# Issue order of the inter-chunk products in the mLSTM part of a hybrid attention/mLSTM layer

## The chip, the cores and the metric

The kernel runs on one core of a Trainium2 chip. A core has five engines with their own instruction streams: TensorE (PE in the profile: matrix products and transposes, with PEld for loading the stationary operand), VectorE (DVE), ScalarE (ACT), GpSimd (POOL) and SyncE (SP), which here issues the DMAs. The engines wait for each other by semaphores. Products land in PSUM, from which VectorE and ScalarE read. The metric is the time of one execution on the device in microseconds; lower is better.

## The reference

One layer of a backbone with 1024 tokens of width 1024 and 256 context tokens. A modulated RMS norm and one input projection feed two head groups: windowed attention (8 query heads, 2 key/value heads, softmax with a sink) and a bidirectional chunkwise mLSTM (4 heads, keys and queries of 64, values of 128). Their outputs are concatenated and projected, and a SwiGLU sub-layer follows. The change is in the mLSTM. Its step for one chunk, cut to what is computed per direction:

```
s   = einsum('bhtd,bhsd->bhts', qc, kc) * w_intra
num = einsum('bhts,bhsv->bhtv', s, vc) + w_inter[..., None] * einsum('bhvd,bhtd->bhtv', C, qc)
den = s.sum(-1) + w_inter * einsum('bhd,bhtd->bht', n, qc)
h   = num / maximum(abs(den), exp(-m_t))[..., None]
```

The first product with `vc` is the intra-chunk part, the one with the carried state `C`, `n` the inter-chunk part. Forward and backward scans are summed.

## The kernel before

The kernel works in tiles of 128 tokens and takes chunks of 128 instead of 64. Its stages are: modulation vectors and input projections; the scan of the mLSTM states; the attention and mLSTM stage, about 290 to 450 us; the output projection; and the SwiGLU sub-layer, with its order written out by hand, to the end.

The attention and mLSTM stage runs over 16 items, one for each of 8 token blocks and 2 groups of four query heads. For an item, `Soft.scores` (L945) makes score products (L954, L955; results in the PSUM tile `s`, two buffers), which VectorE masks and reduces (L956); `Soft.norm` takes the exponential on ScalarE (L965), inverts the sum (L967) and scales on GpSimd (L970). This works two items ahead. `Values` transposes the probabilities (L984, into a PSUM bank called `pt`), splits them into a high and a low part (ScalarE L61, VectorE L62), and adds up products with the values (L994 with the high, L995 with the low part) in `po`; `out` copies and adds (L1002, L1003).

During items 0 to 7 the mLSTM of token block n = 0 to 7 is woven in. `ml_scores(n)` makes the products of keys and queries (L851), two heads at a time: 64 rows each, rows 0 to 63 and 64 to 127 in turn, into two PSUM banks; VectorE multiplies them into the weights `wl` (L856). `ml_values(n, d)`, for direction d = 0 (forward) and 1 (backward), takes two banks, `pv[0]` and `pv[1]`. Head 2j + hb (j and hb from 0 to 1) has its queries and its state in row half hb and adds up in bank `pv[hb]`. So there are four inter-chunk products (L866: scaled queries `qp` times state `cs`, 64 rows, 129 columns, of which the last is the denominator) and four intra-chunk products (L870: `wl` times `V`, 128 rows, 129 columns). Then VectorE makes the denominator (L875, L876 for each half, L877 once for both), and ScalarE (L882, forward) or VectorE (L884, backward) scales the result into `hs`, which frees the banks. `ml_norm` (L891 to L894) and `ml_out` (L900 transposes, L901) finish the block one item later.

All `pt` banks come from one pool of three buffers, so the banks of `ml_values` are those of earlier transposes and of the other direction: a product into a bank waits until what stood there has been read.

The order in this stage is not written out. `PLAN_ML` (L35) gives an order of calls in an item, and a scheduler of the compiler reorders the instructions of each engine by its own cost estimates. `tc.keep_in_program_order(x)` holds instruction x behind the ones that the program wrote before it on its engine. From L1077 on the order is fixed by `tc.manual_schedule()`.

Of the kernel before, what the change touches and what calls it, by code (L numbers as in the profile page):

```python
# [40 lines left out]
def body(tc, x, ctx, vecs, bcv, bada, gqm, gqf, wada, ws1, ws2, wt, wout, wfi, wfo,  # L41
         const, cosc, sinc, out):
    nc = tc.nc
    pe, act, dve, pool = nc.tensor, nc.scalar, nc.vector, nc.gpsimd
# [249 lines left out]
    for sec in (1, 0):  # L294
        pr = [pa.tile([4, 512], F32, name=f"pr{sec}{i}", tag="mm", bufs=4) for i in range(2)]
        for kt in range(KT):
# [17 lines left out]
            for n, (k, a, b) in enumerate(ops):  # L314
                if late and n < 2:
                    prep_t(1, True, (n,))
                for i in range(2):
                    r = pe.matmul(pr[i], a[:, k, :], b[:, i * 512:(i + 1) * 512], start=kt == 0 and n == 0,
                                  stop=kt == KT - 1 and n == len(ops) - 1)
# [19 lines left out]
        r = act.copy(r4[:, 0:512], pr[0])  # L339
# [79 lines left out]
    for i in range(NI):  # L419
# [7 lines left out]
        if i == 0:  # L427
            r = st[:, 13:14]
# [89 lines left out]
    def rows_of(n, d):  # L518
        s_ = n + 2 if d == 0 else 9 - n
        return s_, d * 64 + s_ * 4  # L520
# [166 lines left out]
    def state(d, s_):  # L687
        return c1t[d] if s_ == 1 else cst_[(s_ - 2) // 2][:, (s_ - 2) % 2, d]
# [135 lines left out]
    def bank():  # L824
        return pb.tile([P, 4, P], F32, name="pt", tag="pt", bufs=3)
# [32 lines left out]
    def ml_values(n, d):  # L858
        wt_, qp_, hs = wts[n], qps[n], hss[n][0]
        s_, r0 = rows_of(n, d)  # L860
        cs = state(d, s_)
        pv = [bank().rearrange("p a b -> p (a b)")[:, 0:258].rearrange("p (j v) -> p j v", j=2) for hb in range(2)]
        for j in range(2):
            for hb in range(2):
                r = slice(hb * 64, hb * 64 + 64)
                pe.matmul(pv[hb][:, j, :], qp_[r, d, j, :], cs[r, j, :], start=j == 0, stop=False,  # L866
                          skip_group_check=j > 0)
        for hb in range(2):
            for j in range(2):
                pe.matmul(pv[hb][:, j, :], wt_[:, d, 2 * j + hb, :], V[:, n, 2 * j + hb, :], start=False, stop=True,  # L870
                          skip_group_check=j > 0)
        dn = qa.tile([P, 2, 2], F32, name="dn", tag="dn", bufs=4)
        for hb in range(2):
            den = pv[hb][:, :, 128]
            dve.tensor_tensor(dn[:, hb], den, emcol[:, r0 + hb:r0 + 4:2], MAX)  # L875
            dve.scalar_tensor_tensor(dn[:, hb], den, -1.0, dn[:, hb], MUL, MAX)  # L876
        dve.reciprocal(dn, dn)  # L877
        for hb in range(2):
            for j in range(2):
                t = hs[:, 2 * j + hb]  # L880
                if d == 0:
                    act.activation(t, pv[hb][:, j, 0:128], AF.Copy, scale=dn[:, hb, j:j + 1])  # L882
                else:
                    dve.scalar_tensor_tensor(t, pv[hb][:, j, 0:128], dn[:, hb, j:j + 1], t, MUL, ADD)  # L884
# [149 lines left out]
    for i in range(NIT):  # L1034
# [8 lines left out]
        for k in (PLAN_ML if i < NT else PLAN13 if i == NIT - 3 else PLAN).split():  # L1043
            op, n = k[0], int(k[1:] or 0)
            if op == "w" and i + 1 < NT:
                ml_load(i + 1)
            elif op == "T" and n < b.nt:
                b.tr(n)
            elif op == "M" and n < b.nt:
                b.mm(n)  # L1050
            elif op == "O":
                b.out()
            elif op == "A" and a:
                a.scores(n)
            elif op == "N" and a:
                a.norm(n)
            elif op == "V" and i < NT:
                ml_values(i, n)
            elif op == "x" and i < NT:
                ml_norm(i)  # L1060
            elif op == "s" and i + 1 < NT:
                ml_scores(i + 1)
            elif op == "z" and 1 <= i <= NT:
                ml_out(i - 1)
            elif op == "l":
                for j in WLOADS.get(i, ()):
                    wout_load(j)
            elif op == "p" and 1 <= i <= KT:
                wout_split(i - 1)
            elif op == "m":  # L1070
                msplit(0, 0)
                ops_[0] = pb.tile([P, 1024], F32, name="op", tag="s", bufs=2)
            elif op == "P":
                omm(0, 0, range(n, n + 1))
# [634 lines left out]
    for p in range(4, HT):  # L1709
        j = p - 5  # L1710
# [265 lines left out]
```

## Time and profile before

| what | value |
| --- | --- |
| runs of the kernel, three | 1195.16, 1196.69, 1197.64 us |
| median | 1196.69 us |
| profiled execution, from its first to its last instruction | 1195.1 us |
| TensorE busy | 1174.9 us, 98% |
| VectorE busy | 818.4 us, 68% |
| ScalarE busy | 577.7 us, 48% |
| granted TensorE clock, mean | 0.998 |
| L866 in the trace | 128 records, from 305.1 to 410.6 us |
| L870 in the trace | 128 records, 300 ns in the mean |

Of the profiled execution only the span is given, so the span stands for its time. An fp32 product shows as two records, so the 64 products of L866 are 128 records. The ends of matrix products are modelled, and they overlap; what a product costs is read from one start to the next start. A line of the timeline has its start, its duration, engine, source line, operation, tiles (written <- read), shape and count, and in brackets the idle time before it with what ended it. A line of the chain of work has a start, the time that the chain spent there, and what. The timeline's "x4" merges four records in a row.

### The profile page before, as it was taken

Reading aid. Unit: us, or ns where it says so; the run is one execution under the profiler, and the core shown is the slowest. Engines: PE = TensorE matmul, PEld = TensorE weight load, DVE = VectorE, ACT = ScalarE, POOL = GpSimd, SP = SyncE. Lnnn points to the kernel's source line nnn. Section 1 sums busy time; section 2 is a strip of 40 time slices with the busy share of each in tenths; the row PEclk is TensorE's granted clock in tenths of the full one; section 3 lists DMA queues with packets and bytes.
Section 4 is the critical chain, followed back from the end, with each engine's and each line's share of the span. In section 5 each row is a group of like instructions: output and inputs, shape, how many; then the busy total and the mean of one; then the engine's idle time right before and its main releaser. Section 6 shows DMA issues by size and latency. Waiting matters only on the chain.

```text
span 1195.1 us, 16364 instructions
## 1 busy us (share of the span) xinstructions
PE 1174.9 (98%) x5881; PEld 967.6 (81%) x5881; DVE 818.4 (68%) x1437; ACT 577.7 (48%) x1075; POOL 150.6 (13%) x196
## 2 busy tenths in 40 slices
PE   9899999999999999999999999999999999999997
PEld 3799888877888778888788888888888888888886
DVE  5863768863888895458777678676777656544567
ACT  5743442232777785777534333333333335434443
POOL 1550001215444551000000000000000000000000
PEclk9999999999999999999999999999999999999999
DMA  9522955557878971521133565656553557665853
GB/s 366 193 71 59 374 195 172 179 141 238 191 216 243 313 229 44 203 72 71 63 126 129 203 223 211 206 213 238 203 167 124 200 185 254 206 215 189 303 190 124
DMA packets 104616, 225.37 MB, mean 189 GB/s; under 512 B 10068, under 2 KB 39380, under 8 KB 103128
## 3 DMA queue, kind: packets, MB, share of 16 engines
q1 hardware_dynamic: 104536, 224.34, 56.6%
q8 instruction: 46, 0.75, 0.3%
q14 instruction: 34, 0.28, 0.1%
HBM read 162.43 MB, written 61.21 MB: 187 GB/s over the span
## 4 chain that ended last, share of the span: by engine, by line
PE 80%; DVE 9%; DMA 5%; ACT 2%; issue 2%; POOL 1%; SPq 1%; DVEq 0%; POOLq 0%; ACTq 0%
PE xv L75 8%; PE xv L73 8%; PE xv L74 8%; PE pt L75 6%; PE pt L73 6%; PE pt L74 6%; PE op L73 2%; PE op L75 2%; PE op L74 2%; PE fx L73 2%; PE fx L74 2%; PE fx L75 2%; PE slab L74 2%; PE slab L75 2%; PE slab L73 2%
## 5 line engine op out<-in xcount | busy, mean ns | idle before, releaser
L62 DVE TENSOR_TENSOR fo<-fr,fo 128x1024 fp32r<-128x1024 f32 x77 | 92.6, 1221 | 71.3 <-ACT fo L61 69.5
L61 ACT CAST fo<-fr 128x1024 fp32r<-128x1024 f32 x77 | 79.7, 1051 | 73.9 <-PE pt L75 36.5
L592 PE MATMUL t<-hh,th 128*128 128x512 f32 x208 | 82.4, 396 | 0.0
L593 PE MATMUL t<-hl,th 128*128 128x512 f32 x208 | 81.7, 393 | 0.0
L1382 ACT CAST wS<-wr 128x512 fp32r<-128x512 f32 x88 | 54.2, 622 | 55.4 <-PE pt L75 36.8
L1384 DVE TENSOR_TENSOR wS<-wr,wS 128x512 fp32r<-128x512 f32 x88 | 60.3, 688 | 19.8 <-ACT wS L1382 19.7
L595 PE MATMUL t<-hh,tl 128*128 128x512 f32 x208 | 65.6, 394 | 0.0
L73 PE MATMUL xv<-tT,wS 128*128 128x512 f32 x168 | 65.6, 391 | 0.0
L75 PE MATMUL xv<-tT,wS 128*128 128x512 f32 x168 | 65.6, 391 | 0.0
L74 PE MATMUL xv<-tT,wS 128*128 128x512 f32 x168 | 65.5, 390 | 0.0
L73 PE MATMUL op<-woh,mh 128*128 128x512 f32 x128 | 50.9, 398 | 0.0
L75 PE MATMUL op<-woh,ml 128*128 128x512 f32 x128 | 50.0, 390 | 0.0
L74 PE MATMUL op<-wol,mh 128*128 128x512 f32 x128 | 49.9, 390 | 0.0
L1130 DVE TENSOR_TENSOR wr<-wr 128x512 f32<-128x512 f32 x66 | 45.5, 689 | 1.4
L1416 ACT ACTIVATE es<-es 128x512 f32<-128x512 f32 x22 | 13.9, 633 | 66.6 <-DVE es L1133 66.6
L592 PEld LDWEIGHTS t<-hh,th 128*128 128x128 f32 x208 | 39.1, 188 | 8.3 <-issue 0.3
L593 PEld LDWEIGHTS t<-hl,th 128*128 128x128 f32 x208 | 39.1, 188 | 7.8 <-issue 0.8
L595 PEld LDWEIGHTS t<-hh,tl 128*128 128x128 f32 x208 | 37.4, 188 | 6.9 <-issue 0.7
L73 PE MATMUL pt<-fo 128*128 128x512 f32 x110 | 42.8, 389 | 0.0
L74 PE MATMUL pt<-fo 128*128 128x512 f32 x110 | 42.8, 389 | 0.0
L75 PE MATMUL pt<-fo 128*128 128x512 f32 x110 | 42.8, 389 | 0.0
L954 PE MATMUL s<-k,qh 128*128 128x256 f32 (+1 forms) x128 | 40.9, 329 | 1.0 <-DVE sm L956 0.8
(1013 smaller groups left out, 3407.1 us busy)
## 6 DMA issues: line engine op xcount, KB each, us to landing
wr<-in_wfi SPq DMA_DIRECT2D x44, 512.0 KB, 4.6
wb<-in_wada SPq DMA_DIRECT2D x24, 512.0 KB, 6.3
s_d<-a SPq DMA_DIRECT2D x22, 512.0 KB, 7.0
bt<-in_wfo SPq DMA_DIRECT2D x44, 256.0 KB, 3.7
tb_d<-bt SPq DMA_DIRECT2D x11, 1024.0 KB, 3.9
fr<-s_d SPq DMA_DIRECT2D x44, 256.0 KB, 4.3
fr<-tb_d SPq DMA_DIRECT2D x44, 256.0 KB, 4.3
fr<-a_d SPq DMA_DIRECT2D x33, 256.0 KB, 4.1
```

The source lines that it names most:

```text
L61: act.copy(hi, raw)
L62: dve.tensor_tensor(lo, raw, hi.bitcast(F32), SUB)
L73: pe.matmul(ps, a[0], b[0], start=first, stop=False, **kw)
L74: pe.matmul(ps, a[0], b[1], start=False, stop=False, **kw)
L75: pe.matmul(ps, a[1], b[0], start=False, stop=last, **kw)
L592: pe.matmul(o, wh[:, kt], m[0], start=f, stop=False)
L593: pe.matmul(o, wh[:, kt], m[1], start=False, stop=False)
L595: pe.matmul(o, wl[:, kt], m[0], start=False, stop=l)
L954: pe.matmul(o, qh[:, h, :], k2[g][:, kc], start=True, stop=False)
L1130: dve.tensor_tensor(out, a, b, SUB)
L1382: act.copy(w[:, 0], raw)
L1384: dve.tensor_tensor(w[:, 1], raw, w[:, 0].bitcast(F32), SUB)
```

## The change

The second, third and fourth of the four inter-chunk products of a direction are now held in program order; the first is not held.

```
         for j in range(2):
             for hb in range(2):
                 r = slice(hb * 64, hb * 64 + 64)
-                pe.matmul(pv[hb][:, j, :], qp_[r, d, j, :], cs[r, j, :], start=j == 0, stop=False,
-                          skip_group_check=j > 0)
+                m_ = pe.matmul(pv[hb][:, j, :], qp_[r, d, j, :], cs[r, j, :], start=j == 0, stop=False,
+                               skip_group_check=j > 0)
+                if j or hb:
+                    tc.keep_in_program_order(m_)
         for hb in range(2):
             for j in range(2):
                 pe.matmul(pv[hb][:, j, :], wt_[:, d, 2 * j + hb, :], V[:, n, 2 * j + hb, :], start=False, stop=True,
```

The new lines shift the code behind them by two, so L870 of before is L872 of after, and so on. The written order had the halves in turn before too, but the scheduler put the two products of a half together, with its two intra-chunk products behind them. Of the 16 groups (8 blocks, 2 directions), two now have all four products in a row (blocks 0 and 1, backward); in the other fourteen the first is issued early, by itself, and the three others come in a row behind other work.

TensorE, block 2 forward (`qp_3131` is the block's scaled queries, `wl_3129` its weights, `th__`/`tl__` the split probabilities). Before:

```order
L994 MATMUL po<-th__3227,av_91 128x512
L866 MATMUL pt<-cs_2110,qp_3131 128x129 x2
L870 MATMUL pt<-V,wl_3129 128x129 x2
L995 MATMUL po<-tl__3228,av_91 128x512
L994 MATMUL po<-th__3236,av_91 128x512
L866 MATMUL pt<-cs_2110,qp_3131 128x129 x2
L870 MATMUL pt<-V,wl_3129 128x129 x2
L995 MATMUL po<-tl__3237,av_91 128x512
```

After:

```order
L996 MATMUL po<-th__3227,av_91 128x512
L866 MATMUL pt<-cs_2110,qp_3131 128x129
L997 MATMUL po<-tl__3228,av_91 128x512
L996 MATMUL po<-th__3236,av_91 128x512
L866 MATMUL pt<-cs_2110,qp_3131 128x129 x3
L872 MATMUL pt<-V,wl_3129 128x129 x4
L997 MATMUL po<-tl__3237,av_91 128x512
```

The first product stands alone where the first pair stood, and all intra-chunk products have moved behind the other three.

TensorE, block 2 backward (`s` is the score tile of block 3's `ml_scores`). Before:

```order
L900 MATMUL pt<-vec,hs_2967 128x128 x4
L866 MATMUL pt<-cs_2367,qp_3131 128x129 x2
L870 MATMUL pt<-V,wl_3129 128x129 x2
L851 MATMUL s<-mq_1350,mk_1348 128x128 x2
L851 MATMUL s<-mq_1351,mk_1349 128x128 x2
L866 MATMUL pt<-cs_2367,qp_3131 128x129 x2
L870 MATMUL pt<-V,wl_3129 128x129 x2
```

After:

```order
L902 MATMUL pt<-vec,hs_2967 128x128 x4
L866 MATMUL pt<-cs_2367,qp_3131 128x129
L851 MATMUL s<-mq_1350,mk_1348 128x128 x2
L851 MATMUL s<-mq_1351,mk_1349 128x128 x2
L866 MATMUL pt<-cs_2367,qp_3131 128x129 x3
L872 MATMUL pt<-V,wl_3129 128x129 x4
```

The key-query products L851 have moved ahead of three inter-chunk and all intra-chunk products. Blocks 3 to 5 have the same order; in blocks 6 and 7 four score products of the attention (L954, L955) stand in the place of L851.

VectorE, block 1, from the second reduction of the item's scores to the block's `wl` (`sm` is the second record of a reduction). Before:

```order
L956 ISA pr__3166,sm<-s,mask,bcr 128x640
L956 ISA sm 128x1
L876 SCALAR_TENSOR_TENSOR dn<-pt,dn 128x2
L875 TENSOR_TENSOR dn<-pt,emcol 128x2
L956 ISA pr__3166,sm<-s,mask,bcr 128x640
L956 ISA sm 128x1
L876 SCALAR_TENSOR_TENSOR dn<-pt,dn 128x2
L901 TENSOR_TENSOR mix<-pt,hs_2745 128x512
L1003 TENSOR_TENSOR mix<-po,o_3100 64x512
L956 ISA pr__3166,sm<-s,mask,bcr 128x640
L956 ISA sm 128x1
L877 RECIPROCAL dn<-dn 128x4
```

After:

```order
L958 ISA pr__3166,sm<-s,mask,bcr 128x640
L958 ISA sm 128x1
L877 TENSOR_TENSOR dn<-pt,emcol 128x2 x2
L878 SCALAR_TENSOR_TENSOR dn<-pt,dn 128x2 x2
L879 RECIPROCAL dn<-dn 128x4
L958 ISA pr__3166,sm<-s,mask,bcr 128x640
L958 ISA sm 128x1
L969 RECIPROCAL sm<-sm 128x2
L903 TENSOR_TENSOR mix<-pt,hs_2745 128x512
```

The reciprocal of the forward denominators (L877 before, L879 after) has moved ahead of two reductions and of the two additions. On ScalarE, in the same place, the four L882 of the block have moved from behind the fourth exponential (L965) and the copy L1002 to behind the second exponential. On SyncE some loads of the stage stand a place or two earlier or later; GpSimd's order is the same.

## The prediction

> **What bounds the kernel now.** First the head of the page and its chain of work that ended last, then the source view of the line that changes (L866); line numbers are those of the kernel before.
>
> ```profile
> span 1195.1 us, 16364 instructions
> PE 80%; DVE 9%; DMA 5%; ACT 2%; issue 2%; POOL 1%; SPq 1%; DVEq 0%; POOLq 0%; ACTq 0%
> L866 PE MATMUL pt<-cs,qp x128: 269/272/374, 305.1 to 410.6; 64*128 64x129 f32 x128
> ```
>
> TensorE carries 80% of the chain, so less time on TensorE may shorten the run, but only where the chain really passes through it. L866 runs from 305.1 to 410.6 us, in the eight token blocks of the attention and mLSTM stage. So I read the chain there. First block 0 (columns: start, us on the chain, what):
>
> ```profile
> 305.12 0.64 PE pt L866 x4
> 305.76 0.64 PE pt L870 x4
> ```
>
> TensorE alone is the chain here. One fp32 product is two records, so "x4" is two products. Now block 2, which stands for blocks 2 to 5 (from its first L866 to that of block 3 are 348.71 - 335.04 = 13.7 us):
>
> ```profile
> 335.04 0.64 PE pt L866 x4
> ...
> 341.67 0.67 PE s L851 x8
> ...
> 342.36 0.75 DVE wl L856 x2
> ...
> 347.54 0.50 PE po L995
> ...
> 348.71 0.30 PE pt L866
> ```
>
> The chain leaves TensorE behind L851 and comes back at 347.54, 5.2 us of VectorE and ScalarE later. So what TensorE saves ahead of 341.67 counts only as far as VectorE can start earlier, and what it saves behind that counts for nothing.
>
> **What a product costs, and what two halves cost together.** TensorE's timeline in block 0, backward direction (start, us, what):
>
> ```profile
> 308.91 0.72 PE L851 MATMUL s<-mq,mk 64*128 64x128 f32 x8
> 309.55 0.50 PE L995 MATMUL po<-tl__2903,av 128*128 128x512 f32 x1
> 309.98 0.71 PE L866 MATMUL pt<-cs,qp 64*128 64x129 f32 x4
> 310.62 0.71 PE L870 MATMUL pt<-V,wl 128*128 128x129 f32 x4
> 311.26 0.71 PE L866 MATMUL pt<-cs,qp 64*128 64x129 f32 x4
> 311.90 0.71 PE L870 MATMUL pt<-V,wl 128*128 128x129 f32 x4
> 312.37 0.42 PE L954 MATMUL s<-k,qh 128*128 128x384 f32 x1
> ```
>
> The ends are modelled, so I use start to next start. L866 takes 310.62 - 309.98 = 0.64 us for 4 records, all on one row half. L851 has the same 64-row shape, but its halves take turns, and its 8 records also take 309.55 - 308.91 = 0.64. That is the whole case for the change: two row halves in turn cost what one half costs. How long is one record? Two rows of the chain, with 128x128 transposes:
>
> ```profile
> 334.37 0.44 PE pt L984 x4
> 400.52 0.87 PE pt L984 x8
> ```
>
> Four more records cost 0.43, so one **slot** is 0.11 us. Then 0.64 is 4 slots (0.44) and a fixed 0.20 for going from 128 rows to 64 and back. L870 takes 0.64 where a 64-row product follows, and 312.37 - 311.90 = 0.47 where a 128-row one does; 8 records of it would take 0.47 + 4 x 0.11 = 0.91. Estimates from these rows: a lone product, 2 slots and the fixed part, 0.64 - 0.22 = 0.42; three products with halves in turn, 4 slots, 0.64; four, also 0.64.
>
> The Trainium skill, page "TensorEngine Tiling (Array Packing)", section "Key Properties", says that a change of tiling mode, not of the tile, drains the engine. This speaks against the change, because fourteen of its sixteen groups come out as a lone product, other work, then three. The trace agrees with the rule: the 0.20 above is such a price. If it were zero for the lone product, each forward group would save 0.20 more, 1.6 us over the eight, and the time would be 1190.6 instead of the 1192.2 reached below.
>
> **Forward direction, all eight blocks.** The order now is a lone L866, two value products, three L866, eight records of L870. Before, in block 2:
>
> ```profile
> 334.97 0.71 PE L866 MATMUL pt<-cs,qp 64*128 64x129 f32 x4
> 336.08 0.47 PE L995 MATMUL po<-tl__3228,av 128*128 128x512 f32 x1
> 336.39 0.40 PE L994 MATMUL po<-th__3236,av 128*128 128x512 f32 x1
> 336.72 0.71 PE L866 MATMUL pt<-cs,qp 64*128 64x129 f32 x4
> 337.83 0.48 PE L995 MATMUL po<-tl__3237,av 128*128 128x512 f32 x1
> ```
>
> Before: 337.83 - 334.97 = 2.86. After: 0.42 + 0.34 (L995 to L994, 0.31 here; behind a 64-row product its weights load in the open, between nothing and a slot more, of which I take 0.03, near the short end, as the fixed part already holds such a load) + 0.33 + 0.64 + 0.91 = 2.64. **Saved: 0.22**, and no more, since the lone product pays the fixed part by itself. It lies on the chain: what follows is L954, whose scores VectorE then waits for (0.44 idle before 339.17 below).
>
> **Backward, blocks 2 to 5.** The lone L866 now stands directly ahead of L851, also 64 rows:
>
> ```profile
> 340.32 0.71 PE L866 MATMUL pt<-cs,qp 64*128 64x129 f32 x4
> 341.60 0.71 PE L851 MATMUL s<-mq,mk 64*128 64x128 f32 x8
> 343.16 0.42 PE L954 MATMUL s<-k,qh 128*128 128x384 f32 x1
> ```
>
> Before: 2.84. After: 10 slots and one fixed part, 1.30, then 0.91: 2.21, so 0.63 less on TensorE, and L851 ends about 1 us earlier. What is late next is VectorE:
>
> ```profile
> 339.17 0.89 DVE L956 CUSTOM_DVE_ANT_0 pr__3350<-s,mask,bcr 128x640 f32<-128x640 f32 x1 [0.44 <-PE s L955]
> 341.38 0.67 DVE L1003 TENSOR_TENSOR mix<-po,o 64x512 f32<-64x512 f32 x1
> 342.36 0.75 DVE L856 TENSOR_TENSOR wl<-wl,s 128x256 f32<-128x256 f32 x2 [0.24 <-PE s L851]
> 343.03 0.15 DVE L876 SCALAR_TENSOR_TENSOR dn<-pt,dn 128x2 f32<-128x2 f32 x1
> 343.10 0.74 DVE L856 TENSOR_TENSOR wl<-wl,s 128x256 f32<-128x256 f32 x2
> 343.76 0.16 DVE L967 RECIPROCAL sm<-sm 128x2 f32<-128x2 f32 x1
> 344.49 0.35 DVE L884 SCALAR_TENSOR_TENSOR hs<-pt,dn,hs 128x128 f32<-128x128 f32 x1
> ```
>
> It is busy from 339.17 on but for 0.24. After, L856 follows L1003 at once, at 342.05 instead of 342.36; its four take 1.33 without the L876 between them (342.36 to 343.03 and 343.10 to 343.76); then both L875, both L876 and L877 stand ahead of L884, 0.10 more than the 0.73 from L967 to L884 now: 342.05 + 1.33 + 0.83 = 344.21 against 344.49. I take **0.24** (the 0.10 is my estimate from two operations of 0.15; from 0.10 to 0.30) beside the 0.22. Everything behind L884 moves with it.
>
> **Backward, block 0.** All four together: 312.37 - 309.98 = 2.39 before, 0.64 + 0.91 = 1.55 after, 0.84 less, and VectorE's next L956 waits for exactly these scores. With the forward 0.22 that is 1.06; I take **1.0**, as VectorE's own work then ends within 0.1 of it.
>
> **Block 1.** Here a stall goes. In the chain of work:
>
> ```profile
> 327.39 0.92 ACT pr__3166 L965 x2
> 328.32 0.52 ACT hs L882 x2
> 328.88 0.71 PE pt L866 x4
> ```
>
> The second half of the backward L866 waits for its PSUM bank, which L882 of the forward direction must empty; and L882 stands behind three L956 on VectorE (through L877) and four L965 on ScalarE. Now L877 comes after the second L956 and L882 after the second L965. The two L965 that go behind L882 take 0.92, so L882 starts by 327.4 at the latest, and some 3 us earlier if L877 runs where the order now has it; the four L866 then follow L851 with no wait. L884 has all of VectorE's work ahead of it still, so I don't count the 3 us but about one of them. I take **1.0** with the forward 0.22 in it; bounds 0.22 (nothing but the forward part) and 2.3 (TensorE's 1.06 and two waits, about 1.3).
>
> **Blocks 6 and 7.** L954 lies between the lone L866 and the three, and TensorE's saving is 0.22 again; but VectorE then waits for L870:
>
> ```profile
> 398.22 0.16 DVE L875 TENSOR_TENSOR dn<-pt,emcol 128x2 f32<-128x2 f32 x1 [1.16 <-PE pt L870]
> ```
>
> Now both halves' L875 and L876 come behind its end, about 0.15 more. Net 0.07, with the forward 0.22 **0.3** each.
>
> **At nothing** I cost the DMAs. The order of loads on SyncE's queue changes by a place or two, but the stage's loads are issued about an item before use, and the chain shows none of them inside blocks 2 to 7. If that cover went, a load's landing would show as a DMA link in the chain. GpSimd's order is unchanged.
>
> **Sum:** 1.0 + 1.0 + 4 x (0.22 + 0.24) + 2 x 0.3 = 4.4, I say 4.5. The stages behind have a fixed order and move as a whole. The profiled span is 1195.1, 1.6 below the median of 1196.69 that the runs show; the gain comes off both: 1190.6 and **1192.2**.
>
> **Rivals.**
> 1. TensorE's whole saving counts: 8 x 0.22 + 0.84 x 2 + 4 x 0.63 + 2 x 0.22 = 6.4, and the two waits of block 1, 1.3. Time 1189.0. For it: TensorE's 80% of the chain. Against: VectorE's rows in block 2.
> 2. The halves don't run side by side here, since L866, unlike L851, streams 129 columns and adds up in a bank that L870 goes on with. Then three products take 6 slots and four take 8: 0.22 or 0.44 less per group. Forward nothing is left; block 0 keeps 0.40, block 1 some 0.7, blocks 2 to 5 VectorE's 0.24 each, blocks 6 and 7 lose a little: 1.7, time 1195.0. Against: L851's rows.
> 3. The change does only a part of what it says (two groups of sixteen are four in a row), and the other engines take back what is left: only block 0's gain reaches the end. 1195.7.
> 4. Slower: the first half's products and their L870 now wait until the **second** bank is free too. In block 2 these free it, forward and backward:
>
> ```profile
> 334.68 0.69 DVE L62 TENSOR_TENSOR tl__3237<-pt,th__3236 128x512 fp32r<-128x512 f32 x1
> 338.76 1.14 ACT L882 ACTIVATE hs<-pt,dn 128x128 f32<-128x128 f32 x4 [0.66 <-PE pt L870]
> ```
>
> The three L866 are due at 334.97 + 0.42 + 0.34 + 0.33 = 336.06, 0.69 behind the end of the first (335.37); backward about 1 us behind the end of the second (339.90). One more L956 (0.89) ahead of that L62 makes TensorE wait 0.2, and VectorE's later work comes 0.9 late; if this repeats in every block and reaches L884, a block loses 0.9 and gains 0.55 (a mean of the sum above): 8 x 0.35 = 2.8 slower, 1199.5. It decides from 0.7 us of delay on VectorE, or 1 us on ScalarE. The order shows L956 moved behind, not ahead of, the small operations in block 1, which is against it.
>
> **How the numbers follow.** Forecast 0.56, rival 1 0.13, rival 2 0.12, rival 3 0.10, rival 4 0.08, rest 0.01. "The same" means within 0.2%, 2.4 us, about what a measurement of this kernel can tell from no change. The forecast (by its bounds 1190.5 to 1194.0) and rival 1 are faster, with a little of rival 2: 0.72. Rivals 2 and 3 are the same: 0.20. Rival 4 is slower: 0.08. The range is 1189.0, where all of TensorE's saving ends, to 1195.5, past rival 2; outside are rival 4, most of rival 3 and a little below.
>
> **What would show it.** L866 x6 to its L870 in 0.64 and L866 x8 in 0.64: halves side by side; 0.86 and 1.08 would be rival 2. The lone L866 to the next start in 0.42. L856 in block 2 without idle time before it. L882 in block 1 ahead of L1002, and no L866 waiting for it. Blocks 2 to 5 every 13.2 us instead of 13.7. Any L866 that waits for DVE tl or ACT hs, on the chain, would make this wrong, as would a DMA in the chain of blocks 2 to 7.

## The result, and the profile after

| what | before | after |
| --- | --- | --- |
| median, first sample (4 runs each) | 1196.74 us | 1191.18 us (1190.50 to 1193.09) |
| median, second sample (24 and 6 runs) | 1195.86 us | 1191.67 us (1190.34 to 1195.08) |
| profiled execution | 1195.1 us | 1191.3 us |

The ratio is 0.9961 in the first sample, 95% interval 0.9949 to 0.9972, and 0.9963 (0.9948 to 0.9978) in the second. The change makes the kernel 4.2 to 5.6 us faster by the medians; 4.5 was predicted. Line numbers from L868 on are two higher than before: L870 is now L872, L882 is L884, L954 is L956.

The head of the page of after, its chain by engine, and the source view of L866:

```profile
span 1191.3 us, 16364 instructions
PE 79%; DVE 9%; DMA 6%; ACT 2%; issue 2%; POOL 1%; SPq 1%; DVEq 0%; ACTq 0%; POOLq 0%
L866 PE MATMUL pt<-cs,qp x128: 269/272/375, 304.2 to 403.6; 64*128 64x129 f32 x128
```

The shares say little. What says something is where L866 stands: it began at 305.1 and now begins at 304.2, it ended at 410.6 and now ends at 403.6. So most of the gain arises inside this stage. But the span is only 3.8 shorter, and DMA has a point more of the chain. The chain of work in block 0 of after (start, us, what):

```profile
304.23 0.42 PE pt L866 x2
304.65 0.43 PE po L996
305.08 0.64 PE pt L866 x6
305.72 1.09 PE pt L872 x8
...
308.95 0.65 PE pt L866 x8
309.59 1.09 PE pt L872 x8
```

A lone product takes 0.42, three take 0.64, four take 0.65: six or eight records in what four of one half took before. VectorE in block 2 of after (timeline; start, us, operation, and in brackets idle time ahead):

```profile
336.85 0.69 DVE L903 TENSOR_TENSOR mix<-pt,hs 128x512 f32<-128x512 f32 x1
337.46 0.67 DVE L1005 TENSOR_TENSOR mix<-po,o 64x512 f32<-64x512 f32 x1
338.05 1.40 DVE L856 TENSOR_TENSOR wl<-wl,s 128x256 f32<-128x256 f32 x4
339.38 0.15 DVE L969 RECIPROCAL sm<-sm 128x2 f32<-128x2 f32 x1
339.45 0.20 DVE L877 TENSOR_TENSOR dn<-pt,emcol 128x2 f32<-128x2 f32 x2
```

There is no idle time ahead of L856 any more, and its four run together, as the prediction had it. In the kernel before that idle time (0.24) stood in blocks 2 and 4 only. Block 3 of before, without it:

```profile
355.89 0.16 DVE L875 TENSOR_TENSOR dn<-pt,emcol 128x2 f32<-128x2 f32 x1
356.02 0.75 DVE L856 TENSOR_TENSOR wl<-wl,s 128x256 f32<-128x256 f32 x2
```

**Gains block by block.** A block's gain is how much shorter its stretch is than in the profile of before, from its first L866 to that of the next block (for block 7, to its last L872). For the sum, before's first L866 of block 0 is at 305.05 and its last L870 of block 7 at 411.20; after has 304.16 and 404.67, so 106.15 became 100.51. The columns to the right are from experiments below.

| block | predicted | after | forward only | backward only | backward, not block 1 |
| --- | --- | --- | --- | --- | --- |
| 0 | 1.0 | 1.04 | 0.22 | 0.82 | 0.83 |
| 1 | 1.0 | 1.84 | 1.51 | -2.57 | -0.01 |
| 2, 3, 4, 5 | 0.46 each | 0.55, 0.37, 0.59, 0.37 | 0.24, 0.22, 0.19, 0.23 | 0.40, 0.15, 0.36, 0.17 | 0.39, 0.16, 0.38, 0.15 |
| 6, 7 | 0.3 each | 0.44, 0.45 | 0.22, 0.22 | 0.22, 0.22 | 0.22, 0.21 |
| sum | 4.4 | 5.64 | 3.04 | -0.23 | 2.33 |

The 0.9 by which after is ahead at 305 is not the change's: the stage in which it is made has not begun, and other executions differ by as much there.

**Then 2.6 is given back.** TensorE's instructions run 6.5 earlier than before up to 423, 3.4 to 4.3 earlier from 427 on, and 3.8 earlier in the end. The chain of after there:

```profile
405.82 9.70 DMA ql<-aq_dl
...
415.53 7.97 DMA wor<-in_wout
...
423.58 0.10 ACT woxh L921
...
425.95 0.70 DVE tl__4543 L62
...
426.70 1.12 PE pt L986 x4
```

`wor` is a 128-row piece of the output weights. Each of items 1 to 8 loads one (`wout_raw`), splits it on ScalarE (L921, `woxh`) and GpSimd, stores the parts, and reloads them later. ScalarE's row of after, and of before, for the eighth piece:

```profile
423.58 1.05 ACT L921 CAST woxh<-wor 128x1024 fp32r<-128x1024 f32 x1 [3.63 <-DMA wor<-in_wout]
```

```profile
427.93 1.05 ACT L919 CAST woxh<-wor 128x1024 fp32r<-128x1024 f32 x1 [1.46 <-DMA wor<-in_wout]
```

Softmax and transposes stand behind L921 on ScalarE. It waited 1.46 before and 3.63 now: 2.2 of the 2.6. In this run `wor` was issued 2.4 behind the load of `ql` ahead of it on SyncE, at 415.53, when the `ql` of the chain's first row had landed; in the run of before it was issued 1.3 behind. It then took 8.0 to land instead of 7.0.

TensorE stood idle meanwhile (3.13 ahead of 426.70), and at the end of that its granted clock fell to 0.50. Two stretches of after (us, busy time of PE, PEld, DVE, ACT, POOL with instruction counts, granted TensorE clock, DMA share, GB/s):

```profile
423.30:426.40 3.10, 0.27 (x3) 0.06 (x1) 0.61 (x2) 2.80 (x5) 1.64 (x1) 1.00 0.99 298
426.40:429.80 3.40, 3.10 (x10) 2.61 (x11) 2.76 (x6) 3.37 (x9) 2.41 (x4) 0.50 1.03 334
```

In these 3.4 us TensorE's lead fell by another 1.0, from 4.3 to 3.3. It had that back by 435, in part since a wait of 0.53 in the kernel before is 0.10 here, so the low clock cost nothing in the end at this place. The last 0.4 went at 442, in a wait for VectorE of 0.53 instead of 0.16, whose cause is open.

### The profile page after: what moved, and what is told of

The parts are those of the page before. It is cut to its first block, busy times and chain, and to the rows that moved or that the text cites. A ratio compares the mean times of both kernels' runs of the same rounds, so it can differ in the third digit from the quotient of the medians.

```text
span 1191.3 us, 16364 instructions
## 1 busy us (share of the span) xinstructions
PE 1170.7 (98%) x5881; PEld 963.0 (81%) x5881; DVE 818.9 (69%) x1437; ACT 579.6 (49%) x1075; POOL 151.0 (13%) x196
## 4 chain that ended last, share of the span: by engine, by line
PE 79%; DVE 9%; DMA 6%; ACT 2%; issue 2%; POOL 1%; SPq 1%; DVEq 0%; ACTq 0%; POOLq 0%
PE xv L75 8%; PE xv L73 8%; PE xv L74 8%; PE pt L74 6%; PE pt L75 6%; PE pt L73 6%; PE op L75 2%; PE op L73 2%; PE op L74 2%; PE fx L73 2%; PE fx L75 2%; PE fx L74 2%; PE slab L74 2%; PE slab L75 2%; PE slab L73 2%
## 5 line engine op out<-in xcount | busy, mean ns | idle before, releaser
L956 PE MATMUL s<-k,qh 128*128 128x256 f32 (+1 forms) x128 | 40.9, 329 | 1.1 <-DVE sm L958 0.5
```

What stands on the lines that cost most here:

```text
L956: pe.matmul(o, qh[:, h, :], k2[g][:, kc], start=True, stop=False)
```

## The experiments

Every kernel is compared with runs of the kernel before on the same chip. Those had medians of 1195.86, 1195.79 and 1195.74 in the three batches.

**The same kernel again.** No edit.

> The changed kernel once more, unaltered. In the profiled run of after, block 0 to block 7 of the attention and mLSTM stage gained 5.6 us, and 2.6 of it was given back at 423 to 427 us, where ScalarE's split of the output weights (woxh, L921) waited for the load of wor. Theory A (the 5.6 is the change's, the give-back is a load that lands late and differs from run to run): the stage again gains 5.4 to 5.9; the time behind it gives back between 0 and 3, so 1190 to 1193 in the median. Rival B (the give-back belongs to the change: a stage that ends earlier always meets the same load): the same 2.6 again, at the same place, and a time of 1192 to 1193. Rival C (the 5.6 is itself noise between runs): the stage's gain is off by over 0.5.

1191.67 us, and in the profiled run (1190.87) the stage gained 5.65: the first L866 of block 0 ran 0.38 ahead of before's, the last L872 of block 7 6.03 ahead. Nothing was given back, and TensorE's clock kept 1.00 there. ScalarE's eighth split:

```profile
421.75 1.05 ACT L921 CAST woxh<-wor 128x1024 fp32r<-128x1024 f32 x1 [1.29 <-DMA wor<-in_wout]
```

So the gain in the stage is a property of the program, and the loss behind it differs from run to run (theory A), as far as two profiled runs can tell. The six runs spread over 4.7.

**Forward alone, backward alone.** The condition of the held products, in two kernels:

```
-                if j or hb:
+                if (j or hb) and d == 0:
```

```
-                if j or hb:
+                if (j or hb) and d == 1:
```

> Program order is kept for the forward direction alone; the backward products stand as before. Theory A (the prediction's sum, with block 1 corrected to the 1.8 that after showed, most of it from ScalarE's L884 ahead of two L967): 0.22 in blocks 0 and 2 to 7, about 1.2 in block 1, where L884 stands early as it does in after: 2.7 in the stage, TensorE's lone L866 in 0.42 and three in 0.64. Rival B (a forward group, lone and then three, saves nothing, since the lone product pays the fixed part; all comes from the backward direction): block 1 as in A or less, the others 0, the stage under 1.3. Rival C (L884's place in block 1 is worth nothing by itself): 8 x 0.22 = 1.8. Time by A: before minus 2.7, with up to 2 given back behind the stage.

> Program order is kept for the backward direction alone; the forward products stand as before, and in block 1 ScalarE's L884 stays behind the L967, as in the kernel before. Theory A: 0.84 in block 0 (four together), 0.24 in each of blocks 2 to 5, 0.1 in blocks 6 and 7, and in block 1 at most 0.5, as its backward products still wait for L884: 2.4 in the stage. With the forward part (2.7) the sum is 5.1 to 5.6, so the two halves add up. Rival B (the backward direction carries it): 4.0 or more in the stage, of which block 1 has 1.5 or more. Rival C (VectorE takes all of it back): only block 0's 0.84.

Forward alone: 1193.43, ratio 0.9977 (0.9969 to 0.9986). The table has 0.19 to 0.24 in seven blocks, for which 0.22 was predicted, and 1.51 in block 1. Theory A holds, with block 1 larger than the 1.2 expected of it.

Backward alone: 1195.68, ratio 0.9994 (0.9985 to 1.0002), no gain, where A expected 2.4 in the stage. The table says where: block 1 loses 2.57. TensorE there, in the kernel with backward alone:

```profile
324.15 0.71 PE L851 MATMUL s<-mq,mk 64*128 64x128 f32 x8
324.70 0.41 PE L866 MATMUL pt<-cs,qp 64*128 64x129 f32 x2
327.74 1.23 PE L866 MATMUL pt<-cs,qp 64*128 64x129 f32 x6 [0.60 <-ACT hs L884]
328.89 2.09 PE L872 MATMUL pt<-V,wl 128*128 128x129 f32 x8
330.63 0.67 PE L956 MATMUL s<-k,qh 128*128 128x384 f32 x1
```

And in the kernel before:

```profile
328.88 0.71 PE L866 MATMUL pt<-cs,qp 64*128 64x129 f32 x4 [0.62 <-ACT hs L882]
329.52 0.71 PE L870 MATMUL pt<-V,wl 128*128 128x129 f32 x4
329.99 0.42 PE L954 MATMUL s<-k,qh 128*128 128x384 f32 x1
```

One product goes out at 324.70; the other three wait for the second bank until 327.74, and all eight L872 wait behind them. The kernel before had half of this work (four records each of L866 and L870) out of the way ahead of the wait. And then TensorE is slow: six records in 1.15 (327.74 to 328.89) instead of 0.64, eight L872 in 1.74 (to 330.63) instead of 0.91. Five stretches of the same kernel (us, busy time of PE, PEld, DVE, ACT, POOL with instruction counts, granted TensorE clock, DMA share, GB/s):

```profile
324.70:326.20 1.50, 0.41 (x6) 0.22 (x2) 1.47 (x4) 0.88 (x3) 0.00 (x0) 1.00 0.29 85
326.20:327.70 1.50, 0.86 (x4) 0.65 (x4) 1.50 (x9) 1.45 (x5) 1.25 (x2) 0.86 0.81 239
327.70:331.00 3.30, 3.26 (x15) 3.03 (x16) 0.36 (x3) 0.50 (x2) 1.89 (x3) 0.50 0.52 153
331.00:334.00 3.00, 3.00 (x15) 3.00 (x15) 2.06 (x8) 1.74 (x8) 0.00 (x0) 0.50 0.56 197
334.00:337.00 3.00, 3.00 (x20) 2.44 (x18) 2.76 (x5) 3.00 (x9) 0.98 (x2) 0.98 0.03 5
```

By the 0.86 in the second row and the 0.98 in the last, the granted clock stands at 0.50 from 327.3 to 334.1, 6.8 us, in which TensorE has work nearly all the time; in the 2.6 us ahead of it TensorE was busy for 0.41 + 0.86. How the loss divides was not tried in a run, but the starts allow an estimate. The three products start 9.28 behind the block's first L866 (327.74 - 318.46), no later than the second half in the kernel before (328.88 - 319.60). The scores that follow start 10.39 behind it in the kernel before and 12.17 here. At the full clock's 0.64 + 0.91 they would have started at 10.83. So by these rows the order itself costs some 0.44, and most of the 2.57 is the low clock's. The Trainium skill, page "TensorE: Matmul & The Clock Gate", Part 1, section "What's actually happening", says that an activity monitor halves the clock after an idle window of about 3.4 us. The trace agrees on the half; but here the stretch ahead wasn't empty.

Why the two directions together don't lose this shows on ScalarE, in block 1 of after and of the backward kernel (L884 empties the bank that the three wait for):

```profile
322.24 1.12 ACT L884 ACTIVATE hs<-pt,dn 128x128 f32<-128x128 f32 x4
323.39 0.58 ACT L1004 COPY o<-po 64x512 f32<-64x512 f32 x1
```

```profile
327.08 1.12 ACT L884 ACTIVATE hs<-pt,dn 128x128 f32<-128x128 f32 x4
```

With the forward products held, the scheduler puts L884 ahead of two of the softmax's L967, and the bank is free 4.8 us earlier, or 4.1 if both are reckoned from the block's first L866 (317.68 and 318.46). With the backward products alone it leaves L884 behind them.

**Backward without block 1.**

```
-                if (j or hb) and d == 1:
+                if (j or hb) and d == 1 and n != 1:
```

> The backward direction alone, as in the last run of that kind, but block 1 is left as in the kernel before. With block 1 among them the backward part gained 0.82 in block 0, lost 2.57 in block 1, where all four products and the eight L872 stood behind L884, and gained 1.52 in blocks 2 to 7. Theory A (the loss sits in block 1 alone, and ScalarE's late L884 makes it): block 1 loses at most 0.2, the others gain the same again, 2.3 in the stage, the time 1193 to 1194. Rival B (what block 1 loses is not TensorE's wait but VectorE's order, which the held products change in every block): the later blocks give less than 1.0, and the stage less than 1.5.

1193.61, ratio 0.9985 (0.9977 to 0.9994), 2.33 in the stage, and -0.01 in block 1. The loss sat in block 1 alone. The blocks 0 and 2 to 7 of this kernel and the forward one add up to those of after within 0.07 each. Block 1 doesn't add up: forward alone gains 1.51 and backward alone loses 2.57, but together they gain 1.84.

**Four in a row in the forward direction.** A forward group's first product is held behind the last value product, and in the planner's list the values stand a little earlier:

```
-PLAN_ML = "T0 A0 A1 A2 A3 T1 T2 T3 M0 M1 T4 V0 N0 M2 M3 M4 O z V1 w s N1 x p l"
+PLAN_ML = "T0 A0 A1 A2 A3 T1 T2 T3 M0 M1 T4 N0 M2 M3 V0 M4 O z V1 w s N1 x p l"
...
+                with tc.issue_after(lastmm[0].ins) if d == 0 and not (j or hb) else ExitStack():
+                    m_ = pe.matmul(pv[hb][:, j, :], qp_[r, d, j, :], cs[r, j, :], start=j == 0, stop=False,
...
+            lastmm[0] = pe.matmul(self.po, v2, tl, start=False, stop=t == self.nt - 1)
```

> On top of after: a forward group's first product is held behind the last value product of its block, and the planner's list has N0 and V0 changed in place so that the values stand ahead; the forward groups come out as four in a row, all eight of them, while block 0's backward group becomes a lone product and three. Theory A (the lone product's fixed part is what the change left on the table): a forward group goes from 0.42 + 0.64 to 0.64, 0.42 less on TensorE, on the chain in every block; block 0 loses 0.4 to 0.6; so 2.8 beyond after in the stage (8.4 beyond before), 1189 or less. Rival B (VectorE is the next bound, as the prediction had it for the backward direction in blocks 2 to 5): less than 1 beyond after. Rival C (values and products moved later make VectorE's L875 late): slower than after in the stage.

The stage gained 8.5 over before, as A had it, but the time is 1192.71 (ratio 0.9969, 0.9958 to 0.9980), where A had 1189 or less, and 1.0 above after's median. Behind the stage TensorE falls from 9.0 ahead at 430 to 4.3 ahead at 454 (both by the times of the kernel before). ScalarE's eighth split waits 5.77, by the profile for a reload of split weights (`woh`), which stands behind a store of them on the chain; why L924, which touches only `wor` and `woxh`, should wait for that reload isn't shown:

```profile
421.76 1.04 ACT L924 CAST woxh<-wor 128x1024 fp32r<-128x1024 f32 x1 [5.77 <-DMA woh<-wo_dh]
```

So a shorter stage can run into the output weights' transfers. Its length alone doesn't say by how much: the eighth split waits 1.41 in the forward-only kernel, 0.46 in the backward-only one, and not at all in the one without block 1. The next kernels take these transfers out of the way.

**The output weights one item earlier**, on the kernel before, on after, and on the kernel with four in a row:

```
-        if 1 <= i <= KT + 1:
-            wout_raw(i - 1)
+        if i <= KT:
+            wout_raw(i)
...
-            elif op == "p" and 1 <= i <= KT:
-                wout_split(i - 1)
+            elif op == "p" and i < KT:
+                wout_split(i)
```

> The kernel before, with the output weights' load, split and stores one item earlier throughout (eight items each, starting with item 0), so that the eighth split no longer stands in item 8, where ScalarE's L919 waited 1.46 for the load of wor. Theory A (that load is late in the kernel before already, by about 1 to 1.5 us, which is also the 1.0 that the backward-only run regained behind the stage): 0.5 to 1.5 faster than before. Rival B (it is late only when the stage ends earlier): within 0.5 of before. Rival C (the transfers now meet others earlier in the stage): slower.

> The changed kernel with the same move of the output weights. In the profile of after ScalarE's L921 waited 3.63 in item 8 for the load of wor, and 2.6 of the stage's 5.6 were given back; in the second sample it waited 1.29 and nothing was given back. Theory A (the load's landing is what gives time back, by 0 to 3 us in different runs): no wait of L921 for wor, the 5.6 stands to the end in every run, the median 1.0 to 2.5 below after's and the runs closer together. Rival B (what varies between runs lies elsewhere, in the transfers of q or the weights' reload): the median within 0.5 of after's.

> Four forward products in a row, as before, and the output weights one item earlier. Without the move the stage gained 8.45 over the kernel before, and 4.3 of it was given back at 430 to 436 us, behind the stores and reloads of the output weights. Theory A (the output weights' transfers are the next bound): nearly all of the 8.45 stands to the end, the time 1187 to 1189, the fastest so far. Rival B (the give-back has another cause): 1191 to 1193, as without the move.

Times: 1200.56 on before (ratio 1.0042, 1.0029 to 1.0054), 1194.01 on after (0.9979, 0.9970 to 0.9988), 1190.86 on four in a row (0.9959, 0.9946 to 0.9973). By the times A fails on all three (the third was to take 1187 to 1189). By the traces it holds up to 460: the give-back is gone, and all three even regain 1.7 between 425 and 445, the wait for `wor` that the kernel before had. Then 6.2, 6.4 and 5.0 are lost between 464 and 486. The chain of the kernel with four in a row shows it:

```profile
464.01 0.70 DVE mix L1008
...
464.73 4.51 DMA GTm<-gtm_d
...
469.34 1.29 DVE t L1189
...
472.59 0.80 PE op L75
```

`GTm`, a row that the next stage needs first, is loaded into a buffer from the memory that the attention pool gives up. In after it was issued at 454.83, with no wait:

```profile
454.83 0.42 SPq L1304 DMA_DIRECT2D GTm<-gtm_d  x1
```

Naming `wor` one item earlier moved the pool's buffers, so that VectorE's last read (L1008) now lay on what `GTm` gets. The experiment had a second change in it that I had not seen.

The wait itself is the same in all three, 3.2 to 3.3 us of TensorE. What differs is the clock behind it. On after with the weights early, and on four in a row with the weights early (TensorE's row, then a stretch):

```profile
475.15 0.79 PE L75 MATMUL op<-woh,ml 128*128 128x512 f32 x1 [3.19 <-DVE ml L62]
474.50:481.30 6.80, 6.15 (x15) 4.80 (x16) 1.45 (x3) 3.10 (x5) 0.00 (x0) 0.50 0.98 359
```

```profile
472.59 0.80 PE L75 MATMUL op<-woh,ml 128*128 128x512 f32 x1 [3.28 <-DVE ml L62]
472.10:475.50 3.40, 2.91 (x7) 2.35 (x8) 0.73 (x3) 2.98 (x5) 0.00 (x0) 0.51 1.00 366
```

The kernel before with the weights early has 0.50 for 6.8 us too. Behind the wait, while the clock is low, the three lose another 2.9, 3.0 and 1.5; that is why the third loses 5.0 and the others over 6.

**The same with the buffers where they were.** Ahead of the items, the pool's other buffers are named in the old order:

```
+    for x_, shape, dt_, m in (("dn", (2, 2), F32, 4), ("o2", (4, P), F32, 1), ("sq", (4,), F32, 2),
+                              ("junk", (P,), mybir.dt.bfloat16, 1)):
+        qa.tile([P, *shape], dt_, name=f"{x_}_", tag=x_, bufs=m)
```

> The kernel before, output weights one item earlier, as in the run of that kind that came out 4.8 slower; but the buffers of the attention pool (dn, o2, sq, junk) are named in the old order first, so that GTm's load in the next stage again goes to a buffer that is free early. In the slower run the stage ended 1.65 earlier, as the wait for wor was gone, and then 6.3 was lost at 464 to 480 us, where the load of GTm waited for VectorE's last read of the buffer under it. Theory A (both are so): no GTm link in the chain, 1.0 to 1.7 faster than the kernel before, 1194 to 1195. Rival B (the 6.3 is the price of earlier transfers, wherever the buffer lies): 1199 to 1201 again.

> The changed kernel with the output weights one item earlier and the buffers in the old order. Theory A: the stage's 5.6 and the 1.1 to 1.7 of the wait for wor stand to the end; 6.7 to 7.3 faster than the kernel before, 1188.5 to 1189.5, so the change is worth 5.6 when nothing is given back. Rival B (the transfers set the end of the next stage): 1191 or more.

> Four forward products in a row, output weights one item earlier, buffers in the old order. Theory A: 8.45 in the stage and 1.7 behind it stand to the end, some 10 faster than the kernel before: 1185 to 1187, the fastest. Rival B: 1189 or more, as without the old order of the buffers.

| kernel, weights early, old buffers | median | ratio to before |
| --- | --- | --- |
| before | 1195.08 us | 0.9995 (0.9986 to 1.0004) |
| after | 1189.57 us (1189.02 to 1189.93) | 0.9950 (0.9938 to 0.9963) |
| four in a row | 1186.14 us (1185.91 to 1187.23) | 0.9925 (0.9911 to 0.9938) |

The loss at `GTm` is gone in all three. Between the first two lies the change by itself, with the output weights out of its way: 1195.08 - 1189.57 = 5.5, as the stage's 5.6 says. The runs of after lie within 0.9 instead of 4.7; but these are runs on another chip, on which the kernel before lies within 2.3 instead of 4.3, so that the weights did this isn't shown. The kernel with four in a row lies in A's 1185 to 1187; after lies 0.07 above A's 1188.5 to 1189.5. On the kernel before the earlier weights regain 1.66 in the profiled run, but the medians differ by 0.7 only, not told apart from nothing; A's 1.0 to 1.7 isn't confirmed there. Four in a row now keeps its 8.45: 9.6 below before, the fastest version of all, 5.0 below the median of after in its first sample.

**Does the turn of the halves matter?** The fastest version with the two loops exchanged, so that both products of rows 0 to 63 stand ahead of both of rows 64 to 127:

```
-        for j in range(2):
-            for hb in range(2):
+        for hb in range(2):
+            for j in range(2):
```

> The same as the last, but the four products stand half by half (both products of the first row half, then both of the second) instead of the halves in turn; in the forward direction all four are still adjacent. In the backward direction they fall apart into two pairs. Theory A (two halves in turn cost what one costs; adjacency alone gives nothing): a forward group of eight records takes 8 slots and the fixed part, 1.08 instead of 0.64, on the chain: 8 x 0.44 = 3.5 lost forward, and backward up to 1.5 more; 1188.5 to 1191. Rival B (the gain comes from standing adjacent, with one change of row mode instead of two; the halves don't matter): 0.64 for eight records, and no more than 1.5 lost, from the backward direction.

Block 1, forward, with halves in turn and then half by half:

```profile
321.27 0.71 PE L869 MATMUL pt<-cs,qp 64*128 64x129 f32 x8
321.92 1.16 PE L875 MATMUL pt<-V,wl 128*128 128x129 f32 x8
```

```profile
321.35 0.72 PE L869 MATMUL pt<-cs,qp 64*128 64x129 f32 x8
322.00 1.16 PE L875 MATMUL pt<-V,wl 128*128 128x129 f32 x8
```

Both take 0.65 for eight records. My theory A (1.08) falls, and B's 0.64 holds. Half by half, the records start in pairs 14 ns apart, where two records of one half start 0.11 us apart. The trace doesn't name a record's half, but by this spacing the second half runs beside the first, though all of the first half stand ahead of it in the program. So the order within the group doesn't matter; that no 128-row instruction stands between the halves does. The kernel comes out at 1188.03, 1.9 above the one with halves in turn, where B had allowed 1.5, and its stage gains 6.59 instead of 8.45: the backward groups fell apart into pairs again. Block 2, backward:

```profile
336.63 0.71 PE L869 MATMUL pt<-cs,qp 64*128 64x129 f32 x4
337.26 0.71 PE L875 MATMUL pt<-V,wl 128*128 128x129 f32 x4
```

Four records of one half take 0.63 there. Blocks 2 to 7 lose 0.39, 0.15, 0.39, 0.16, 0.21 and 0.23, which is what the backward products had gained in them (the table's last column).

## Why the prediction was right, and where it wasn't

1192.2 was forecast, 1191.18 measured. The step sizes behind it, one by one:

- **Price of a product**: right. 0.42 for a lone one, 0.64 for three, 0.65 for four; eight L872 in 0.91 (on the timeline of after from 305.65 to the next start at 306.56). Rival 2 (halves one after the other) is refuted. But the step "two row halves in turn cost what one half costs" named the wrong condition: in turn or not, they run side by side.
- **Forward 0.22**: right, 0.19 to 0.24 in seven blocks of the forward-only kernel.
- **Block 0, 1.0**: right, 1.04.
- **Block 1, 1.0**: too small, 1.84. The step that failed is "I don't count the 3 us but about one of them". The forward-only kernel alone gets 1.51, which is its 0.22 and all of the 1.3 that stood in the bounds for the two waits. The backward products then add 0.33, not TensorE's whole 0.84.
- **Blocks 2 to 5, 0.46**: right in the mean, (0.55 + 0.37 + 0.59 + 0.37) / 4 = 0.47. The backward part is 0.27 by the kernel without block 1, beside the 0.24 taken for VectorE. But block 2 doesn't stand for blocks 2 to 5, as the prediction had it: the backward part is 0.39 and 0.38 in blocks 2 and 4, 0.16 and 0.15 in blocks 3 and 5. The 0.24 of idle time ahead of L856, which the change removed, stood in blocks 2 and 4 of the kernel before only (block 3's rows are shown above). So the agreement of the mean is in part luck.
- **Blocks 6 and 7, 0.3**: too small, 0.44 and 0.45. TensorE's backward 0.22 counts in full; the 0.15 that I took off for the later L875 and L876 wasn't there.
- **"At nothing I cost the DMAs"**: wrong, and against the gain. The prediction looked at blocks 2 to 7, where the chain has none; but the eighth piece of the output weights belongs to item 8, behind block 7, and the kernel before already waited 1.46 for it. A stage that ends 5.6 earlier gives back 0 there in one profiled run and 2.6 in another. With the weights one item earlier nothing is given back.

So the terms came out at 5.64 instead of 4.4, and between 0 and 2.6 was lost behind them: two errors of opposite sign. In the second sample (4.2 gained) they nearly cancel, and that 4.5 comes so close to it is luck; in the first (5.6) nearly the whole of the stage's gain shows, and the forecast of the time is 1.0 too high.

Rival 1 (TensorE's whole saving, 7.7 in the stage) is refuted: 5.64. Rival 3 is refuted by the blocks. Rival 4 (the second bank is late) didn't happen in the change, but it is real: backward alone is that case, in block 1, at 2.57 for a single block instead of the 0.9 I put on it, most of it by the low clock, which rival 4 did not have. It stayed away since the forward part moved L884; the reason given, that L956 moves behind the small operations there, agrees with this.

The sentence on the lone product's fixed part can be judged too: it put 0.20 on a forward group, and being rid of the lone product is worth more. Four in a row gains 8.45 - 5.65 = 2.8 beyond after in the stage, with block 0's backward group split in exchange. From the backward group of block 2 to that of block 7 its fastest version gains 4.91 on before (from 336.34 to 399.37, where before has 340.32 to 408.26), after 2.32 (336.33 to 401.95): 0.52 more in each of five blocks, beside an estimate of 0.42 for the lone product, its fixed part and its two slots.

## What to carry to other kernels

Products that use half of TensorE's rows are to stand adjacent, both halves within one group and nothing of 128 rows between them; the order within the group is free here. But a group that waits for two PSUM banks waits for the later one with everything behind it, so look first at who empties that bank: the same edit gained 0.3 or lost 2.6 in one block, by where another engine's reading of the bank stood. When TensorE waits for some 3 us, look at its granted clock behind the wait too: the low clock cost up to 3.0 here, beside a wait of 3.2. And when a stage gets shorter, read the waits for loads behind its end: what is 1.5 late now can take back part of the gain, in some runs more than in others. A buffer that is named at another time can move the next stage's loads behind another reader.

## What the runs showed of the hardware that I had not expected

- Two row halves run side by side although all four records of the one stand ahead of all of the other in the program: 0.65 for eight, starts in pairs 14 ns apart. The Trainium skill, page "TensorEngine Tiling (Array Packing)", section "Key Properties", says that tiles operate independently; this run agrees, and adds that they needn't take turns.
- TensorE's granted clock fell to 0.50 in the middle of the kernel, for 3.4 or 6.8 us, in six of the profiled runs, each time while TensorE waited: from 327.3 to 334.1 with backward alone, after 2.6 us in which it was busy for 1.27; from 426.4 to 429.8 in after, after 3.1 us with 0.27; from 422.9 to 429.7 with four in a row; and behind the wait for `GTm`, where the 3.4 or 6.8 us at 0.50 cost 1.5 or 3 beside a wait of 3.2. In block 1 the kernel before waits in the same place, 0.30 and 0.62 instead of 1.16 and 0.60, and keeps 1.00.
- The wait for one load differs between two executions of the same program by more than 2 us (3.63 and 1.29). It may carry part of the spread between runs, but this isn't shown: the six runs of after reach from 1190.34 to 1195.08, the five with that load an item earlier from 1189.02 to 1189.93, on another chip.
